# Combinations from kept scaled activations, a gate read by halves, adaLN in lots of eight and another order of the last down tiles in a two-layer trunk

## The chip, the core and the metric

The kernel runs on one core of one Trainium2 chip. The metric is the device time of one execution in microseconds; a profile of one execution stands beside it. The engines are TensorE (PE in the rows; PEld is its weight load), VectorE (DVE), ScalarE (ACT), GpSimd (POOL) and SyncE (SP), which issues all DMAs. On-chip buffers are SBUF tiles and, for TensorE's results, PSUM banks, here two accumulators of two banks each (`acc`) and four single banks (`aux`).

## The reference, cut to what matters

Two layers act on 512 prompt positions and 8 decode positions, 520 columns of width 1024, all in fp32. Each layer has an FFN at half weight, a mixing of a gated delta rule with windowed attention, and a second FFN. Each of the three begins with an RMS norm with shift and scale and ends with a gate; the nine vectors per layer come from a conditioning vector:

```python
m = jax.nn.silu(c) @ w_ada + b_ada                      # adaLN: 9 x 1024 per layer
h = rms_norm(x, g) * (1.0 + scale) + shift              # _modulate
x = x + 0.5 * gate * ((silu(h @ w_g) * (h @ w_u)) @ w_down)     # FFN, d_ff = 2816
h = modulate(x); x = x + gate * (mix(h @ w_in) @ w_out)         # mixing
```

The prompt has one set of the nine vectors for all its positions, the decode rows have one each.

## The kernel before

**Numbers and tiles.** x lies with its width on the partitions: 8 tiles k of 128 rows, each with 520 columns. The columns come in two halves (`HALF`): half 0 has 256 prompt columns, half 1 has 256 prompt and 8 decode columns, 264. Every fp32 matrix product is done as three matmuls on rounded parts: the high part of one factor by the high part of the other and the two mixed terms (`mmk`). So each activation h has a tile `hh` and a tile `hl` (high and low), one set for each half, and each 128x512 piece of a weight a `whi`, made by ScalarE, and a `wlo`, made by VectorE. Loads of 128x1024 (`raw`, a ring of four) and these pieces (a ring of eight) are run by `Stream`.

**Order.** There is no loop on the chip. The program is written out by one planner: `Clock` keeps an estimated time for each engine, and `Fill` holds side jobs written as generators (a norm, the combinations, adaLN lots), and starts a step of one of them between matmuls when the estimate says that its inputs are ready. The cost figures in `Ops` (lines 315 to 361) only decide this order. Every engine then executes its own row of instructions in that order, and waits where the first in the row waits.

**An FFN** (`ffn`, line 789). The norm of its input (`Norm`) makes `rs` from the sum of squares `ss`, one half at a time, and then for each of the 8 tiles k: VectorE forms t = x·g·rs, ScalarE rounds t + shift to `hh`, and VectorE forms `hl`. t alternates between two borrowed buffers, so the rows show them as `sq` and `ss`. For half 1 the 8 decode columns are done ahead of all this (`hs`). `head` (line 656) then makes the first two gate tiles and the first two up tiles in the plain way: 96 matmuls on half 0 into the accumulators, and 96 on half 1 into the four `aux` banks. The products of the other columns of d_ff, 128 gate columns and 128 up columns at a time, are made with a two by two scheme of seven products instead of eight (`seven`; 78 of them in the program). It needs sums of weights (GpSimd, `sum`, four per seven), and it needs combinations of h over the two halves and over tiles k and k + 4: for h1 = (tile k of half 0, of half 1) and h2 = (tile k + 4 of both),

```python
y0 = [h1[1] - h1[0],  h2[1] - y0[0]]
y1 = [h2[1] - h1[1],  h2[0] - y0[1]]
```

with k from 0 to 3. `combine` (line 762) makes them. GpSimd first adds `hh` and `hl` to a full h (`h32`; 4 operations of 128x264 per k), VectorE forms the four differences, ScalarE rounds y0 and y1 to `th` and VectorE forms their low parts `th`. `head` gives the job a turn after each of its 32 products. In `ffn` the results of `head` then go to `gate`, which reads an accumulator and an aux bank of each of its tiles; `seven` takes two aux banks and half of an accumulator.

The 22 tiles of d_ff are worked in two parts of 11 (`PARTS`), each with its sevens and then a down stage, in which the products with w_down are added to x. In the second part the last two tiles of x (y and z, numbers 6 and 7) are done by `tail` (line 722) with the halves apart, so that the norm of the next sub-layer can begin with half 0. It takes them as (0, y), (1, y), (0, z), (1, z), where the first number is the half. Its 11 tiles of d_ff make 33 matmuls per item.

**adaLN** (`ada_gen`, line 489) is a side job. One vector needs two lots of eight 256 KB loads, so four groups of four loads; the job keeps two groups in flight. The four products of a group show in the trace as one row of 8 records (`aux<-ada,sc`), and after the fourth group ScalarE copies the bank (`ada_sb`), TensorE transposes it and VectorE adds it up into `mt`. Outside the sevens it takes an aux bank; during them (`pairs`) it takes an accumulator for its whole vector.

## Time and profile before

| | us |
|---|---|
| median of three runs | 2313.55 |
| lowest and highest of them | 2308.82 and 2315.8 |
| the profiled execution's own time | 2309.65 |
| its span, from first to last instruction | 2307.9 |
| TensorE busy in it | 2158.9 (94%) |
| VectorE busy | 1657.3 (72%) |
| ScalarE busy | 1116.8 (48%) |
| GpSimd busy | 627.4 (27%) |

The mean granted clock of TensorE is 0.970 of full speed. A row of a timeline gives the start, the duration, the engine, the line and operation, the tile written and the tiles read, and the count of like instructions taken together; in brackets behind it stands the time that the engine was idle before it, and what ended that. Matmuls overlap, so their durations (0.28 us) are longer than the distance from one to the next.

### The profile page before, as it was taken

Reading aid. Unit: us, or ns where it says so; the run is one execution under the profiler, and the core shown is the slowest. Engines: PE = TensorE matmul, PEld = TensorE weight load, DVE = VectorE, ACT = ScalarE, POOL = GpSimd, SP = SyncE. Lnnn points to the kernel's source line nnn. Section 1 sums busy time; section 2 is a strip of 40 time slices with the busy share of each in tenths; the row PEclk is TensorE's granted clock in tenths of the full one; section 3 lists DMA queues with packets and bytes.
Section 4 is the critical chain, followed back from the end, with each engine's and each line's share of the span. In section 5 each row is a group of like instructions: output and inputs, shape, how many; then the busy total and the mean of one; then the engine's idle time right before and its main releaser. Section 6 shows DMA issues by size and latency. Waiting matters only on the chain.

```text
span 2307.9 us, 44270 instructions
## 1 busy us (share of the span) xinstructions
PE 2158.9 (94%) x17218; PEld 2018.2 (87%) x17218; DVE 1657.3 (72%) x3278; ACT 1116.8 (48%) x2438; POOL 627.4 (27%) x451
## 2 busy tenths in 40 slices
PE   7899999999988979999996999999999888899999
PEld 5789889989977868987996999999988777899999
DVE  5874687566877887567749956965677769974982
ACT  4453355356744445334534644643657444652651
POOL 0540452000111244044304614610001203532630
PEclk8999999999999989999997999999999998999999
DMA  8663454343223356358321333333432242233332
GB/s 277 231 223 105 175 182 140 110 78 104 85 74 118 124 177 216 110 205 303 105 93 46 97 105 95 98 107 98 87 108 67 79 131 74 84 107 94 93 109 75
DMA packets 177538, 287.79 MB, mean 125 GB/s; under 512 B 50448, under 2 KB 96176, under 8 KB 177328
## 3 DMA queue, kind: packets, MB, share of 16 engines
q1 hardware_dynamic: 177328, 284.96, 39.2%
q8 instruction: 135, 2.21, 0.4%
q14 instruction: 75, 0.61, 0.1%
HBM read 271.55 MB, written 14.41 MB: 124 GB/s over the span
## 4 chain that ended last, share of the span: by engine, by line
PE 79%; DVE 13%; ACT 4%; issue 2%; DMA 1%; SPq 0%; POOL 0%; DVEq 0%; ACTq 0%
PE aux L317 40%; PE acc L317 38%; DVE y L352 2%; DVE wlo L352 2%; DVE hl L352 1%; DVE sq L352 1%; ACT whi L344 1%; PE aux L327 1%; DVE th L352 1%; DVE ss L352 1%; ACT sq L344 1%; DVE g L352 1%; ACT s L344 1%; DVE s L352 1%; DVE x L352 1%
## 5 line engine op out<-in xcount | busy, mean ns | idle before, releaser
L344 ACT ACTIVATE whi<-raw 128x512 fp32r<-128x512 f32 (+1 forms) x594 | 360.1, 615 | 427.1 <-PE acc L317 303.2
L352 DVE TENSOR_TENSOR wlo<-raw,whi 128x512 fp32r<-128x512 f32 (+1 forms) x594 | 431.8, 744 | 71.8 <-ACT whi L344 71.2
L361 POOL TENSOR_TENSOR sum<-raw 128x512 f32<-128x512 f32 x156 | 247.2, 1585 | 848.3 <-DMA raw<-in_gu 664.1
L317 PE MATMUL aux<-th,whi 128*128 128x264 f32 (+1 forms) x2496 | 467.5, 286 | 3.7 <-ACT u L344 3.6
L317 PEld LDWEIGHTS aux<-th,whi 128*128 128x128 f32 x2496 | 384.8, 188 | 27.3 <-issue 13.4
L317 PE MATMUL aux<-th,wlo 128*128 128x264 f32 (+1 forms) x1248 | 353.3, 283 | 0.0
L352 DVE TENSOR_TENSOR wlo<-sum,whi 128x512 fp32r<-128x512 f32 x312 | 335.3, 1106 | 19.0 <-ACT whi L344 16.6
L317 PE MATMUL acc<-hh,whi 128*128 128x256 f32 x1256 | 326.0, 301 | 19.0 <-DVE x L352 14.7
L317 PE MATMUL acc<-hl,whi 128*128 128x256 f32 x1256 | 306.3, 285 | 6.7 <-DVE hl L352 6.3
L317 PE MATMUL acc<-hh,wlo 128*128 128x256 f32 x1256 | 305.9, 285 | 6.7 <-DVE wlo L352 6.7
L317 PE MATMUL aux<-hl,whi 128*128 128x264 f32 x928 | 269.2, 290 | 32.0 <-DVE hl L352 32.0
L317 PE MATMUL aux<-hh,whi 128*128 128x264 f32 x928 | 273.0, 294 | 11.8 <-ACT g L344 11.8
L317 PE MATMUL acc<-ghi,whi 128*128 128x256 f32 (+1 forms) x1320 | 272.4, 282 | 7.9 <-DVE t L352 7.9
L317 PE MATMUL acc<-glo,whi 128*128 128x256 f32 (+1 forms) x1320 | 272.0, 282 | 0.0
L317 PE MATMUL acc<-ghi,wlo 128*128 128x256 f32 (+1 forms) x1320 | 271.8, 282 | 0.0
L317 PE MATMUL aux<-hh,wlo 128*128 128x264 f32 x928 | 268.4, 289 | 0.0
L317 PEld LDWEIGHTS acc<-hh,whi 128*128 128x128 f32 x1256 | 220.3, 192 | 54.5 <-issue 37.0
L352 DVE SCALAR_TENSOR_TENSOR x<-acc,mt,x 128x256 f32<-128x256 f32 x136 | 61.6, 480 | 244.2 <-PE acc L317 244.2
L317 PEld LDWEIGHTS aux<-th,wlo 128*128 128x128 f32 x1248 | 234.8, 188 | 0.0
L317 PEld LDWEIGHTS acc<-hl,whi 128*128 128x128 f32 x1256 | 219.3, 192 | 8.3 <-DVE hl L352 7.9
L317 PEld LDWEIGHTS acc<-hh,wlo 128*128 128x128 f32 x1256 | 219.2, 191 | 8.1 <-DVE wlo L352 8.0
L344 ACT ACTIVATE whi<-sum 128x512 fp32r<-128x512 f32 x312 | 193.9, 623 | 46.6 <-PE acc L317 43.1
(318 smaller groups left out, 4014.4 us busy)
## 6 DMA issues: line engine op xcount, KB each, us to landing
raw<-in_gu SPq DMA_DIRECT2D x176, 512.0 KB, 3.6
...
```

Of the source, the lines that this page charges most:

```text
L317: self.nc.tensor.matmul(out, lhsT=lhsT, rhs=rhs, start=start, stop=stop, skip_group_check=join)
L327: self.nc.tensor.transpose(out, in_, ident)
L344: self.nc.scalar.activation(**k)
L352: getattr(self.nc.vector, f)(**k)
L361: getattr(self.nc.gpsimd, f)(**k)
```

## The change

1. **Combinations.** `Norm` of an FFN keeps t of all eight tiles and both halves (`ht`, 128x2x264), instead of overwriting it. Eight columns of half 0, which have no prompt position, are zero, and the eight decode columns of half 1 hold hs less the prompt's shift. `combine` forms differences of these t on GpSimd (three operations per k: y0[0], d, y1[1]) as soon as tile k + 4 of half 1 has its t (`norm.made`), and VectorE adds the shifts in two `stt` per k (y0[1], y1[0]) when the whole norm is done. The `h32` tiles are gone.
2. **The gate of the head.** `head` takes a generator `early`, which does the activation and the product of half 0 while half 1's matmuls run; half 1 follows in `gate_rest`, its splitting to high and low parts later. The first two sevens use the head's accumulators. A seven otherwise takes one aux bank and a whole accumulator. `head` offers `combine` a turn after every second product.
3. **adaLN.** Lots of eight loads instead of four, and always an aux bank. The side job may now go on in the down stage of the first part (`spares`).
4. **The last down tiles** come as (0, y), (0, z), (1, y), (1, z).
5. The planner's cost of GpSimd rises from 0.0019 to 0.003 us per column.

```diff
-        self.clk.run("pool", 0.1 + 0.0019 * self.cols(k["out"]), [k["out"]], self.aps(k, ("in_", "in0", "in1")))
+        self.clk.run("pool", 0.1 + 0.003 * self.cols(k["out"]), [k["out"]], self.aps(k, ("in_", "in0", "in1")))
...
-    def ada_load(l, g, h):
+    def ada_load(l, g):
         t = []
-        for k in range(4 * h, 4 * h + 4):
+        for k in range(KD):
             a = slot("ada", F32, (128, 512))
             dma(out=a, in_=ada[l, g, k])
...
+    def ada_mm(t, pa, u):
+        for k in range(KD):
+            r = 32 * (k % 4)
+            mm(pa[r:r + 32], lhsT=sc[:, u, k, :], rhs=t[k], start=u == 0 and k < 4, stop=u == 1 and k > 3, frac=0.27)
...
-            return len(used) + 4 <= SLOTS - 13
+            return len(used) + KD <= SLOTS - spares[0]
...
-            if not u and not h:
-                if pairs[0]:
-                    pa, pt = (acc()[:, i] for i in range(2))
-                else:
-                    pa, pt = aux(), None
-            ada_mm(t, pa, u, h)
-            if u and h:
+            if not u:
+                pa = aux()
+            ada_mm(t, pa, u)
+            if u:
                 m_sb = ada_out(pa)
                 yield m_sb,
...
             gg = mt[l][:, (3 * j + 1) * 8:(3 * j + 1) * 8 + 8, :]
-            t = [q[:, o:o + 256] for q in (self.sq, self.ss)]
+            keep = j != 1
+            if keep and a == 0:
+                self.ht = [slot("ht", F32, (128, 2, 264)) for _ in range(KD)]
+                for q in self.ht:
+                    pool("memset", out=q[:, 0, 256:264], value=0.0)
+            if keep:
+                t = [q[:, a, 0:256] for q in self.ht]
+            else:
+                t = [q[:, o:o + 256] for q in (self.sq, self.ss)] * 4
...
+                    if keep:
+                        for k in range(k0, k1):
+                            pool("tensor_tensor", out=self.ht[k][:, 1, 256:264], in0=hs[:, k - k0],
+                                 in1=sh[:, k, 0:1].to_broadcast([128, NS]), op=ALU.subtract)
+                elif keep:
+                    ops.copy(out=h8, in_=s0_)
+                    tt(out=l8, in0=s0_, in1=h8.bitcast(F32), op=ALU.subtract)
...
-    def head(norm, e=None):
+    def head(norm, e=None, early=None):
...
         norm.need(1, 0)
+        early = early(banks[0]) if early else None
         b1 = [aux() for _ in range(4)]
...
-                fill.try_(e)
+                if i % 2:
+                    fill.try_(e)
+            if early and k:
+                next(early, None)
...
     def combine(norm, th):
         for k in range(4):
-            yield lambda: norm.done[1] >= k + 5
-            h1, h2 = (slot("h32", F32, (128, 2, 264)) for _ in range(2))
-            for t, kk in ((h1, k), (h2, k + 4)):
-                for a in range(2):
-                    pool("tensor_tensor", out=t[:, a], in0=hh[a][0][:, kk, :].bitcast(F32),
-                         in1=hh[a][1][:, kk, :].bitcast(F32), op=ALU.add)
-            yield h1, h2
+            yield lambda: norm.made[1] >= k + 5
             y0, y1 = (slot("y", F32, (128, 2, 264)) for _ in range(2))
-            tt(out=y0[:, 0], in0=h1[:, 1], in1=h1[:, 0], op=ALU.subtract)
-            tt(out=y1[:, 0], in0=h2[:, 1], in1=h1[:, 1], op=ALU.subtract)
-            tt(out=y0[:, 1], in0=h2[:, 1], in1=y0[:, 0], op=ALU.subtract)
-            tt(out=y1[:, 1], in0=h2[:, 0], in1=y0[:, 1], op=ALU.subtract)
+            d = slot("d", F32, (128, 264))
+            h1, h2 = ht[k], ht[k + 4]
+            pool("tensor_tensor", out=y0[:, 0], in0=h1[:, 1], in1=h1[:, 0], op=ALU.subtract)
+            pool("tensor_tensor", out=d, in0=h2[:, 1], in1=h2[:, 0], op=ALU.subtract)
+            pool("tensor_tensor", out=y1[:, 1], in0=y0[:, 0], in1=d, op=ALU.subtract)
...
+        yield lambda: norm.done[1] >= KD
...
+            stt(out=y0[:, 1], in0=h2[:, 1], scalar=sh[:, k + 4:k + 5], in1=y0[:, 0], op0=ALU.add, op1=ALU.subtract)
+            stt(out=y1[:, 0], in0=h2[:, 1], scalar=ds[:, k:k + 1], in1=h1[:, 1], op0=ALU.add, op1=ALU.subtract)
...
+            pa, pb, pc = banks.pop(0) if banks else (None, aux(), None)
+            if pa is None:
                 u = acc()
-                unit.extend((u[:, 0], u[:, 1]))
-            pa = unit.pop(0)
+                pa, pc = u[:, 0], u[:, 1]
+            if pb is None:
+                pb, pc = aux(), aux()
...
+        def early(banks):
+            for i in range(0, 4, 2):
+                t = slot("g")
+                half.append(t)
+                act(out=t[:, 0:256], in_=banks[i], func=AF.Silu)
+                yield
+                tt(out=t[:, 0:256], in0=t[:, 0:256], in1=banks[i + 1], op=ALU.mult)
+                yield
+        def gate_rest(t, pg, pu):
+            act(out=t[:, 256:520], in_=pg, func=AF.Silu)
+            tt(out=t[:, 256:520], in0=t[:, 256:520], in1=pu, op=ALU.mult)
+            later(*split(t))
...
-                items = [(0, y, True, True, True), (1, y, False, False, True), (0, z, True, True, True), (1, z, False, False, True)]
+                items = [(0, y, True, True, True), (0, z, True, True, True), (1, y, False, False, True), (1, z, False, False, True)]
```

How the built kernels' rows differ is shown at three places. The first is VectorE in the head of the second FFN. Here `y` are the differences, `th` the low parts of the rounded ones, `wlo` low parts of weights, `hl` the low parts of h. Before, from the first combination's weights on:

```order
L352 TENSOR_TENSOR wlo_9578<-raw_9241,whi_9577 128x512
L352 TENSOR_TENSOR wlo_9581<-raw_9241,whi_9580 128x512
L352 TENSOR_TENSOR wlo_9587<-sum_9408,whi_9586 128x512
L352 TENSOR_TENSOR y_9620<-h32_9599 128x264
L352 TENSOR_TENSOR y_9621<-h32_9600,h32_9599 128x264
L352 TENSOR_TENSOR y_9620<-h32_9600,y_9620 128x264
L352 TENSOR_TENSOR y_9621<-h32_9600,y_9620 128x264
L352 SCALAR_TENSOR_TENSOR hl1_77<-sq_7639,mt0_80,hh1_76 128x256
L352 TENSOR_TENSOR th_9627<-y_9620,th_9626 128x528
L352 TENSOR_TENSOR th_9629<-y_9621,th_9628 128x528
L352 TENSOR_TENSOR y_9660<-h32_9651 128x264
```

After, from the last three `hl` on:

```order
L352 SCALAR_TENSOR_TENSOR hl1_77<-ht_9052,mt0_80,hh1_76 128x256
L352 SCALAR_TENSOR_TENSOR hl1_77<-ht_9053,mt0_80,hh1_76 128x256
L352 TENSOR_TENSOR dsh_9563<-mt0_80 128x4
L352 SCALAR_TENSOR_TENSOR y_9539<-ht_9050,mt0_80,y_9539 128x264
L352 SCALAR_TENSOR_TENSOR y_9540<-ht_9050,dsh_9563,ht_9046 128x264
L352 SCALAR_TENSOR_TENSOR y_9545<-ht_9051,mt0_80,y_9545 128x264
L352 SCALAR_TENSOR_TENSOR y_9546<-ht_9051,dsh_9563,ht_9047 128x264
L352 TENSOR_TENSOR th_9568<-y_9539,th_9567 128x528
L352 TENSOR_TENSOR th_9570<-y_9540,th_9569 128x528
L352 SCALAR_TENSOR_TENSOR y_9551<-ht_9052,mt0_80,y_9551 128x264
L352 SCALAR_TENSOR_TENSOR y_9552<-ht_9052,dsh_9563,ht_9048 128x264
L352 TENSOR_TENSOR th_9606<-y_9545,th_9605 128x528
```

The last two `hl` of half 1 stood between rows of the combinations (the second of them further on); now the first difference comes behind the last `hl`, and a `y` on VectorE reads `ht` instead of `h32`.

The second is GpSimd in the same head; before, `h32` is the sum of the two parts of h:

```order
L361 TENSOR_TENSOR h32_9512<-hh0_74,hl0_75 128x264
L361 TENSOR_TENSOR h32_9512<-hh1_76,hl1_77 128x264
L361 TENSOR_TENSOR h32_9513<-hh0_74,hl0_75 128x264
L361 TENSOR_TENSOR h32_9513<-hh1_76,hl1_77 128x264
L361 TENSOR_TENSOR sum_9584<-raw_9241,raw_9285 128x512
L361 TENSOR_TENSOR sum_9590<-raw_9241,sum_9408 128x512
L361 TENSOR_TENSOR h32_9599<-hh0_74,hl0_75 128x264
L361 TENSOR_TENSOR h32_9599<-hh1_76,hl1_77 128x264
L361 TENSOR_TENSOR h32_9600<-hh0_74,hl0_75 128x264
```

After, where `ht` are the kept scaled activations:

```order
L361 TENSOR_TENSOR ht_9053<-hs_9468,mt0_80 128x8
L361 TENSOR_TENSOR y_9539<-ht_9046 128x264
L361 TENSOR_TENSOR d_9541<-ht_9050 128x264
L361 TENSOR_TENSOR y_9540<-y_9539,d_9541 128x264
L361 TENSOR_TENSOR y_9545<-ht_9047 128x264
L361 TENSOR_TENSOR d_9547<-ht_9051 128x264
L361 TENSOR_TENSOR y_9546<-y_9545,d_9547 128x264
L361 TENSOR_TENSOR y_9551<-ht_9048 128x264
L361 TENSOR_TENSOR d_9553<-ht_9052 128x264
L361 TENSOR_TENSOR y_9552<-y_9551,d_9553 128x264
L361 TENSOR_TENSOR y_9557<-ht_9049 128x264
```

The four additions per k have become three subtractions, which stand in one row, ahead of the weight sums of the next seven.

The third is VectorE at the entry of the first mixing, behind the first FFN's last down tiles (`x` written from `acc` is half 0, from `aux` half 1). Before:

```order
L352 SCALAR_TENSOR_TENSOR x_73<-aux_5364,mt0_80,x_73 128x256
L352 TENSOR_TENSOR t8_5415<-aux_5364,mt0_80 128x8
L352 TENSOR_TENSOR x_73<-x_73,t8_5415 128x8
L352 TENSOR_TENSOR ss_4765<-ss_4765,sq_4766 128x264
L352 SCALAR_TENSOR_TENSOR x_73<-acc_5420,mt0_80,x_73 128x256
L352 TENSOR_TENSOR ss_4765<-ss_4765,sq_4766 128x256 x2
L352 TENSOR_TENSOR wlo_5409<-raw_5264,whi_5408 128x512
L352 SCALAR_TENSOR_TENSOR sq_4766<-x_73,mt0_80,rs_5484 128x256
L352 SCALAR_TENSOR_TENSOR ss_4765<-x_73,mt0_80,rs_5484 128x256
L352 SCALAR_TENSOR_TENSOR hl0_75<-sq_4766,mt0_80,hh0_74 128x256
```

After:

```order
L352 SCALAR_TENSOR_TENSOR x_73<-acc_5331,mt0_80,x_73 128x256
L352 TENSOR_TENSOR ss_4773<-ss_4773,sq_4774 128x256
L352 SCALAR_TENSOR_TENSOR x_73<-acc_5331,mt0_80,x_73 128x256
L352 TENSOR_TENSOR ss_4773<-ss_4773,sq_4774 128x256 x2
L352 TENSOR_TENSOR wlo_5333<-raw_5180,whi_5332 128x512
L352 SCALAR_TENSOR_TENSOR sq_4774<-x_73,mt0_80,rs_5437 128x256
L352 SCALAR_TENSOR_TENSOR ss_4773<-x_73,mt0_80,rs_5437 128x256
L352 SCALAR_TENSOR_TENSOR hl0_75<-sq_4774,mt0_80,hh0_74 128x256
L352 SCALAR_TENSOR_TENSOR sq_4774<-x_73,mt0_80,rs_5437 128x256
```

The second half-0 tile (`acc_5331`) now comes ahead of the first half-1 tile, and with it the first rows of half 0's norm (`sq` from `x` and `rs`).

## Rows read from the trace of the kernel before

**Rows 1.** The page's chain that ended last, shares of the span by engine.
```profile
PE 79%; DVE 13%; ACT 4%; issue 2%; DMA 1%; SPq 0%; POOL 0%; DVEq 0%; ACTq 0%
```

**Rows 2.** TensorE's waits: line, waited for: us in total, times, longest us.
```profile
PE aux L317 <- DVE hl L352: 32.0, 6, 8.5
...
PE aux L317 <- ACT g L344: 17.7, 3, 5.9
...
PE aux L327 <- ACT ada_sb L344: 8.0, 2, 7.3
...
PE acc L317 <- DVE t L352: 7.9, 7, 1.1
...
PE acc L317 <- DVE wlo L352: 6.7, 5, 3.8
...
PE acc L317 <- DVE hl L352: 6.3, 3, 2.4
```

**Rows 3.** Timeline of PE, head 2: start, us, operation, [idle before <-releaser].
```profile
812.31 0.59 PE L317 MATMUL aux<-hl,whi 128*128 128x264 f32 x1 [8.46 <-DVE hl L352]
...
817.65 0.59 PE L317 MATMUL aux<-hl,whi 128*128 128x264 f32 x1 [2.33 <-DVE hl L352]
...
826.33 1.94 PE L317 MATMUL aux<-ada,sc 128*32 128x512 f32 x8 [5.89 <-ACT g L344]
```

**Rows 4.** Windows of head 2: us, busy (records) by engine, PEclk, DMA share, GB/s.
```profile
794.80:804.00 9.20, 9.05 (x75) 8.84 (x73) 9.02 (x13) 2.26 (x5) 6.09 (x7) 1.00 0.03 10
812.30:820.50 8.20, 5.80 (x23) 5.18 (x23) 8.17 (x10) 1.88 (x4) 6.86 (x6) 0.50 0.04 14
835.00:845.00 10.00, 10.00 (x86) 8.88 (x88) 9.00 (x11) 5.55 (x12) 6.05 (x4) 1.00 0.87 315
```

**Rows 5.** Timeline of DVE, head 2.
```profile
790.67 0.23 DVE L352 TENSOR_TENSOR hs<-x,rs 128x64 f32<-128x64 f32 x1 [1.55 <-ACT rs L344]
...
810.29 0.42 DVE L352 TENSOR_TENSOR y<-h 128x264 f32<-128x264 f32 x1
...
820.73 1.49 DVE L352 TENSOR_TENSOR y<-h,h 128x264 f32<-128x264 f32 x1
...
826.03 0.42 DVE L352 TENSOR_TENSOR g<-g,acc 128x256 f32<-128x256 f32 x1 [0.98 <-ACT g L344]
...
830.19 1.32 DVE L352 TENSOR_TENSOR th<-y,th 128x528 fp32r<-128x528 f32 x2
```

**Rows 6.** Timeline of POOL, head 2, and its 128x8 memsets (line, busy, mean ns).
```profile
798.20 0.75 POOL L361 TENSOR_TENSOR h<-hh,hl 128x264 f32<-128x264 f32 x1 [3.11 <-DVE hl L352]
...
820.59 1.33 POOL L361 TENSOR_TENSOR sum<-sum,raw 128x512 f32<-128x512 f32 x1
...
L967 POOL MEMSET bt<- 128x8 f32 x2 | 0.2, 104 | 0.0
```

**Rows 7.** Timeline of PE, the last product on th of head 2's first seven.
```profile
837.76 0.28 PE L317 MATMUL aux<-th,wlo 128*128 128x264 f32 x1
```

**Rows 8.** Windows of the three entries behind an FFN, columns as in rows 4.
```profile
450.00:470.00 20.00, 14.13 (x98) 13.46 (x99) 17.67 (x44) 9.88 (x21) 0.00 (x0) 0.91 0.36 112
1204.90:1224.10 19.20, 15.33 (x116) 14.36 (x116) 16.60 (x36) 10.42 (x21) 2.97 (x4) 1.00 0.17 55
1591.70:1610.70 19.00, 14.44 (x101) 13.61 (x101) 17.03 (x44) 9.73 (x22) 0.00 (x0) 0.91 0.37 118
```

**Rows 9.** Timeline of PE, entry of the first mixing.
```profile
464.07 0.39 PE L317 MATMUL acc<-hh,wlo 128*128 128x256 f32 x1 [3.76 <-DVE wlo L352]
```

**Rows 10.** Timeline of DVE there, half 0's last hi/lo half.
```profile
459.38 0.48 DVE L352 SCALAR_TENSOR_TENSOR hl<-ss,mt,hh 128x256 fp32r<-128x256 f32 x1 [0.18 <-ACT hh L344]
```

**Rows 11.** Timelines of PE and ACT, adaLN's transposes in the first FFN.
```profile
94.85 1.11 PE L327 MATMUL aux<-cs,ada_sb 128*128 128x128 f32 x4 [7.31 <-ACT ada_sb L344]
...
94.22 0.58 ACT L344 ACTIVATE ada_sb<-aux 128x512 f32<-128x512 f32 x1
```

**Rows 12.** Timeline of SP, adaLN loads in the first FFN.
```profile
71.53 13.43 SPq L311 DMA_DIRECT2D ada<-in_ada  x16
```

100 lines of the change are left out of this document (63 added, 37 removed).

## The prediction

> **What bounds the kernel now.** I read the chain of waits first: it runs through TensorE for 79% of the span and through VectorE for 13% [rows 1]. So TensorE sets the time, and what can be won is its idle time and the stretches in which it runs slowly. The list of TensorE's waits comes next [rows 2]. The matrix products themselves are not changed in number, so only waits can go. Six lines of that list belong to places that the diff touches: hi/lo halves of h that VectorE hands over late (32.0 us in 6 waits), the gate's activation (17.7 us in 3), an adaLN copy (8.0 us), accumulators in the down stage (7.9 us in 7), a late weight half (6.7 us) and hi/lo halves at the entry of the mixing (6.3 us). Of these 78.6 us nearly all is within the edit's reach; the few small waits in the groups I leave.
>
> The three heads with a full queue (the second to fourth FFN) all look the same, which the counts 6 and 3 show. I take head 2. TensorE stands still for 8.46, 2.33 and 5.89 us [rows 3], and between and behind these waits it crawls: 12 matmuls lie between the starts at 812.31 and 817.65, so without the 2.33 us of waiting they take 3.01 us, 0.25 us each. In the stretch before the first wait 75 matmuls take 9.05 us, 0.121 each, at a granted clock of 1.00; in the stretch behind it the clock is 0.50, the lower of the two levels (1.2 GHz) [rows 4]. So after each idle time there is a further loss of some microseconds.
>
> Why TensorE waits: VectorE is the queue in front of it. From 790.67 (the first row of the second half's norm) to 826.03 (the gate's product) it is busy nearly without a break, 9.02 of 9.20 us and 8.17 of 8.20 us in two stretches [rows 4, 5], and the hi/lo half that TensorE waits for until 812.31 stands behind eight differences y, two halves th and three weight halves, as the order of the kernel before shows. Those rows are also slow: a y of 128x264 took 0.42 us at 810.29, while GpSimd had nothing to do, and 1.49 us at 820.73, while a sum of 1.33 us ran on GpSimd [rows 5, 6]. VectorE and GpSimd hinder each other there.
>
> **The heads.** The change takes 4 of 16 additions per head from GpSimd and 8 of 16 differences from VectorE, lets GpSimd begin when the scaled activations exist (not when both halves of h are split), and puts all 16 norm instructions ahead of the combinations. Now count VectorE's instructions. Before, 46 stand from the norm's first row to the gate's product, and they take 826.03 - 790.67 = 35.4 us, 0.77 each [rows 5]. After, the hi/lo halves of h are within the first 22, so the 96 matmuls of the second half, which need 96 x 0.121 = 11.6 us from 794.8, run through to about 806.4, without waiting for the aux buffers of the gate. The first thing that TensorE then needs from VectorE is the 35th instruction, a weight half (at 0.77 each: 817.6), and the last combination is the 44th: 790.7 + 44 x 0.77 = 824.5. The last 9 of the 36 products on it need 1.1 us; since TensorE will have idled from some 809 to 817 it restarts at the lower clock, and I allow 1 to 2 us more: 827. Before, these 36 products ended at 838.0 [rows 7]. That gives 11 us per head, 33 for three. This is the largest and the least certain term. The lower end: if GpSimd's twelve operations in a row hold VectorE back as at 820.73 most of the time, the mean rises to 1.0 us per instruction, the 44th ends at 834.7 and the head gains 1 to 2 us, 4 in all. The upper end: the rows are undisturbed, 0.55 us each, the 44th ends at 815, and TensorE (806.4 plus 12 + 12 + 36 matmuls at 0.121 and some 3 us for 16 adaLN records and the transposes, 10 us and a little) sets the end near 818: 20 per head, 60 in all. I choose the middle because the work per instruction stays mixed in the same way, and the measured mean contains the contention.
>
> The Trainium skill, page "SBUF — State Buffer", section "SBUF: two separate sides", says that the port pair shared by VectorE and GpSimd is an exclusive lock, so that a VectorE operation with two SBUF inputs and a GpSimd operation exclude each other for whole instructions. The 1.49 us beside 0.42 us agrees with that. The rule speaks against this change, since the new `stt` still read two SBUF operands and GpSimd's twelve operations now start amid the norm's sixteen. With full exclusion the undisturbed rows add up: 8 th at 0.66 and 36 others at 0.42 us on VectorE, 12 operations at 0.75 and six sums at 1.33 us on GpSimd [rows 5, 6], together 37.4 us; the last combination would stand at 828.1 instead of 824.5, and the time would be 11 us longer over three heads, 2261.
>
> The early gate of half 0 costs nothing on ScalarE, which is free for most of the head; it takes the 5.89 us wait apart, which is inside the count above. The extra 8 memsets and 8 tiny differences of 128x8 on GpSimd per norm stand ahead of the big ones; a memset of 128x8 takes 0.104 us [rows 6], so together under 2 us of a queue that has nothing else to do then. At the opening two more small VectorE operations per group: under 1 us.
>
> **The entries behind the FFNs.** Moving half 0's last tile ahead of half 1's lets half 0's norm start 33 matmuls earlier, 33 x 0.121 = 4.0 us. Before, in the three stretches between the end of the last down tile and the second half's first matmul, TensorE works 98, 116 and 101 records, at 0.121 us 11.9, 14.0 and 12.2 us, in 20.0, 19.2 and 19.0 us [rows 8]: losses of 8.1, 5.2 and 6.8, together 20.1. The largest single wait of the first is 3.76 us for a weight half that stood on VectorE behind half 1's first norm rows [rows 9]; the lower clock adds to it (0.91 in the mean). The last hi/lo half of half 0 ends at 459.86 [rows 10]; 4 us earlier it ends near 456, and the first half, which wants it at 450.0 + 7 x 1.43 = 460.0, does not wait. The weight half now stands ahead of half 0's last rows. In its place the last two hi/lo halves of half 1 stand behind three weight halves that wait for buffers which half 1's fourth step frees; each row of that kind takes 0.48 us [rows 10], so I count 0 to 1 us an entry. I count 20.1 - 3 = 17. Lower end 6, if VectorE, 17.67 of 20.00 us busy there [rows 8], only changes which half is late; upper end 20.
>
> **The first FFN.** TensorE's transposes wait 7.31 us for an adaLN copy on ScalarE that stands at 94.22 behind four copies y to th, which wait for VectorE [rows 11]. After, no such copy stands between others that wait, and the products come later than the copies. The wait goes, with some of the lower clock behind it. Against that, the loads come in one row of 24 at about 0.84 us each (16 took 13.43 us [rows 12]), and the first lot of eight may land 2 us after TensorE wants it. I count 6.5; ends 0 and 9.
>
> **The down stage of the first FFN.** Seven waits of 1.13 us, 7.9 in all [rows 2], are for one accumulator less: the adaLN lot in flight held one of the two, and now it takes an aux buffer. I count 7; the ends are 4 (two lots that now run in this stage keep TensorE waiting 2 us each, about two of these waits) and 7.9.
>
> **Sum.** 33 + 17 + 6.5 + 7 = 63.5 us. The profiled execution took 2309.65 us, the median of the runs is 2313.55. From the profiled one this gives 2246, from the median 2250. I forecast 2250. The lower ends add to 14, the upper to 97; they will not fall together.
>
> **Rivals.**
> (1) The wait at the heads only moves: TensorE stops waiting for h and waits as long for a combination or a weight half. For it: VectorE was full, and only 2 of 46 instructions leave the row before the last combination. Against: eight differences and four additions are gone. It gives 4 for 33: 2279. Chance 0.13.
> (2) The heads run undisturbed, 60 for 33: 2223. Chance 0.10; the contention in [rows 5] speaks against it.
> (3) Slower: weights late behind lots of eight. SP issues all loads in one order, and a lot is now 8 x 256 KB, 2.1 MB, which at the 315 GB/s of a busy stretch [rows 4] takes 6.7 us, 3.3 longer than half a lot. If each of the 32 lots keeps TensorE 3.3 us longer from a weight, that is 106 us, and the time is 2250 + 106 = 2356; from 20 lots on (63.5 / 3.3 = 19.2) the change is slower than before. For it: the DMA engines are 0.87 busy in that stretch. Against: 16 loads in a row are issued now too [rows 12], the list of TensorE's waits has no wait for a raw weight, and the total of bytes is the same. Chance 0.05.
> (4) The entries gain nothing but the order: 6 for 17, and the opening 0 for 6.5: 2267. Chance 0.12.
> That the new order does not come about is no rival: the order of the built kernel shows it.
>
> **How the numbers follow.** The forecast's own case, 2238 to 2264, has 0.60, the rivals 0.40. The range 2226 to 2282 leaves out the slow rival, half of rival 2 and a little beyond rival 1, some 0.15 to 0.2. What a measurement of this kernel can tell from no change is 0.3%, 7 us. Every case but the third is faster by more than that, and a mix of the lower ends (14) with a mild form of rival 3 would lie within it: faster 0.91, same 0.04, slower 0.05.
>
> **What would show it.** Right: in head 2 no wait for `hl` among the 96 matmuls of the second half, one wait of 5 to 10 us before the products on th, and these ending 9 to 13 us sooner relative to the second half's start; no seven waits on `t`; no 7.31 us for `ada_sb`; entries of 12 to 14 us. Wrong: new waits for `ada` or raw loads by DMA among TensorE's waits (rival 3), a wait for `th` as long as the three of before (rival 1), or y rows on VectorE well over 1 us. What I don't see from here is what the changed planner cost does to later stages of the mixing; I take that as nothing.

## The result and the profile after

The changed kernel took 2285.43 us (median of four runs, 2283.64 to 2285.63), the kernel before 2311.95 on the same occasions: a ratio of 0.9883, with an interval of 0.9866 to 0.9900. The change gains 27 us, less than half of the 63.5 that were forecast, and the time lies 3.4 us above the upper end of the range. The profiled execution took 2285.49 us, at a mean granted clock of 0.979; against the profiled one of before it is 24.2 us shorter (23.8 between the marks used below).

From the page of the changed kernel, the busy time of each engine and the chain that ended last:

```profile
PE 2155.7 (94%) x17218; PEld 2022.2 (89%) x17218; DVE 1602.5 (70%) x3264; ACT 1119.0 (49%) x2438; POOL 603.5 (26%) x499
...
PE 76%; DVE 16%; issue 3%; ACT 3%; DMA 1%; SPq 0%; POOL 0%; DVEq 0%; ACTq 0%
```

VectorE has 55 us less work than before (1657.3), GpSimd 24 less. Yet VectorE's share of the chain rose from 13% [rows 1] to 16%: where TensorE waits, it still waits for VectorE's row. TensorE's waits in the changed kernel (waited for: us in total, times, longest us), to be read beside [rows 2]:

```profile
PE acc L317 <- DVE x L352: 17.6, 12, 3.5
PE acc L317 <- ACT u L344: 15.9, 10, 11.6
...
PE acc L317 <- DVE g L352: 12.8, 15, 3.1
PE acc L317 <- ACT g L344: 9.2, 1, 9.2
PE acc L317 <- DVE hl L352: 8.1, 5, 3.7
PE acc L317 <- DVE wlo L352: 7.9, 4, 3.7
PE aux L317 <- DMA ada<-in_ada: 6.4, 1, 6.4
...
PE aux L317 <- DVE hl L352: 2.7, 4, 1.4
...
PE aux L327 <- ACT ada_sb L344: 0.7, 1, 0.7
```

The old names are nearly gone: `aux <- hl` fell from 32.0 to 2.7 us, `ada_sb` from 8.0 to 0.7, and the seven waits on `t` do not appear. New names have come: ScalarE's copies `u` and `g`, and VectorE's product `g` 15 times. The largest entry, for `x`, stood in the list of before with 14.7 us in 8; four waits of 0.7 us have been added, one in each tail. (The 6.4 us for `ada` is the opening's, which before had one of its own of 6.3.)

To see where the time went I cut both traces at marks that exist in both and compared the distances, in us:

| part | forecast | before to after |
|---|---|---|
| heads of the second, third, fourth FFN | -33 | -6.4, -5.1, -6.2: -17.7 |
| three entries behind an FFN | -17 with the next | -7.3, -2.2, -5.9: -15.3 |
| four tails | | +1.4, -0.3, +0.9, +1.2: +3.2 |
| head of the first FFN, from its start to the last product on th | -6.5 | +0.2 |
| sevens and first down stage of the first FFN | -7 | -9.2 |
| late part of the two mixings, up to the next norm | 0 | +8.7, +4.9: +13.5 |
| sevens and first down stage, second FFN | 0 | -3.8 |
| the same, third and fourth FFN | 0 | +3.6, +1.8: +5.3 |
| all else | 0 | -0.1 |
| sum | -63.5 | -23.8 |

Each distance is from one execution of each kernel; some vary by 2 to 4 us, as the experiments show. Of the 39.7 us that are missing, the heads account for 15.3, the late mixings for 13.5, the first FFN's head for 6.7, entries and tails for 4.9, and the sevens nearly cancel (-0.7).

**Heads.** VectorE did what was forecast and a little more. In head 2 the row from `hs` (784.50) to the last `th` (end 815.22) takes 30.7 us; 33.8 were forecast up to the last combination. In heads 3 and 4 it takes 30.9 and 31.8. The ends of that row in head 2, on VectorE:

```profile
784.50 0.23 DVE L352 TENSOR_TENSOR hs<-x,rs 128x64 f32<-128x64 f32 x1 [2.91 <-ACT rs L344]
...
813.90 1.32 DVE L352 TENSOR_TENSOR th<-y,th 128x528 fp32r<-128x528 f32 x2
```

But the end of the products on th came not 2.5 us after it, as allowed, but 10.3, 9.5 and 8.1 us. None of the 36 products started before the last combination was made, and in head 3 TensorE stood idle until then. Timelines of the changed kernel, first PE and then ACT and DVE, around that wait:

```profile
1221.40 0.27 PE L317 MATMUL acc<-hh,wlo 128*128 128x256 f32 x1
1233.29 0.81 PE L317 MATMUL acc<-th,whi 128*128 128x264 f32 x2 [11.61 <-ACT u L344]
...
1236.77 0.81 PE L317 MATMUL acc<-th,whi 128*128 128x264 f32 x2 [0.48 <-ACT u L344]
```

```profile
1227.13 1.18 ACT L344 ACTIVATE th<-y 128x528 fp32r<-128x528 f32 x2 [2.01 <-DVE y L352]
1229.18 1.18 ACT L344 ACTIVATE th<-y 128x528 fp32r<-128x528 f32 x2 [0.87 <-DVE y L352]
...
1232.34 0.62 ACT L344 ACTIVATE ghi<-g 128x520 fp32r<-128x520 f32 x1
1232.86 0.37 ACT L344 ACTIVATE u<-acc 128x264 f32<-128x264 f32 x1
```

TensorE's next product writes an accumulator that ScalarE must empty first (`u`). That copy needs nothing from VectorE: its product was done at 1221.7. But it stands in ScalarE's row behind copies `th<-y`, and each row of those waits for VectorE's `y`. So the row that was to be hidden is waited for in full here. The forecast counted VectorE's row and TensorE's work, and ScalarE as "free for most of the head"; free it is, but not free to go on. In heads 2 and 4 the longest waits are 2.09 and 3.13 us for the gate's `g`, which VectorE and ScalarE make behind rows of the combinations. The 24 plain products of the first seven follow these waits (in head 2 with adaLN products between them, in head 4 mostly at the lower clock), and the products on th come last.

ScalarE is not the only reason. In `seven` the 36 products stand on TensorE as three runs of 12, and each run goes through all four combinations. So 26 of the 36 stand behind the last combination's low part, not 9. The kernel before shows the same: its last `th` of head 2 ends at 831.51 [rows 5], and the first product on th (PE, before) starts behind that. They end 6.5 us after the last `th` in head 2 and 5.1 in heads 3 and 4, so 2.5 us was too little by the trace of before already.

```profile
832.31 0.41 PE L317 MATMUL aux<-th,whi 128*128 128x264 f32 x2
```

Two smaller things in the same places. A weight half now waits behind norm rows of half 1 at the start of heads 2 and 4; and after each such wait TensorE runs at the lower clock. PE and DVE of the changed kernel, start of head 2, and two windows (us, busy (records) by engine, PEclk, DMA share, GB/s): the 6 us behind this wait, and the 5 us behind the wait of 11.61:

```profile
788.83 0.58 PE L317 MATMUL acc<-hh,wlo 128*128 128x256 f32 x1 [3.68 <-DVE wlo L352]
```

```profile
787.54 1.23 DVE L352 TENSOR_TENSOR wlo<-raw,whi 128x512 fp32r<-128x512 f32 x1
```

```profile
788.80:794.80 6.00, 5.97 (x28) 5.98 (x29) 6.00 (x10) 2.03 (x4) 4.16 (x5) 0.50 0.92 344
1233.30:1238.30 5.00, 4.52 (x19) 4.21 (x20) 5.00 (x9) 2.71 (x6) 0.16 (x1) 0.50 0.40 119
```

28 matmuls in 6.0 us are 0.21 each, against the 0.121 at full clock.

**First FFN.** The wait for `ada_sb` [rows 11] is gone, and one of 9.24 us for the gate's `g` ends 13 us earlier. Timelines of PE, ACT, DVE and POOL of the changed kernel:

```profile
81.48 0.80 PE L317 MATMUL acc<-hh,whi 128*128 128x256 f32 x2 [9.24 <-ACT g L344]
```

```profile
72.48 0.64 ACT L344 ACTIVATE th<-y 128x528 fp32r<-128x528 f32 x1 [1.80 <-DVE y L352]
73.97 0.64 ACT L344 ACTIVATE th<-y 128x528 fp32r<-128x528 f32 x1 [0.85 <-DVE y L352]
78.73 0.64 ACT L344 ACTIVATE th<-y 128x528 fp32r<-128x528 f32 x1 [4.11 <-DVE y L352]
80.23 0.64 ACT L344 ACTIVATE th<-y 128x528 fp32r<-128x528 f32 x1 [0.85 <-DVE y L352]
80.78 0.65 ACT L344 ACTIVATE g<-acc 128x256 f32<-128x256 f32 x2
```

```profile
68.08 0.48 DVE L352 SCALAR_TENSOR_TENSOR y<-ht,dsh 128x264 f32<-128x264 f32 x1
...
77.21 1.49 DVE L352 SCALAR_TENSOR_TENSOR y<-ht,mt,y 128x264 f32<-128x264 f32 x1
78.62 1.51 DVE L352 SCALAR_TENSOR_TENSOR y<-ht,dsh 128x264 f32<-128x264 f32 x1
```

```profile
78.48 1.36 POOL L361 TENSOR_TENSOR sum<-sum,raw 128x512 f32<-128x512 f32 x1
```

It is the same pattern as in head 3: an activation whose input is ready stands behind copies that wait for VectorE, and VectorE's rows take three times their undisturbed 0.48 us, as long as the sums on GpSimd beside them.

**Late mixing.** Behind the first mixing's middle a wait of 3.68 us for `hl` is new. PE and DVE of the changed kernel:

```profile
701.79 0.39 PE L317 MATMUL acc<-hl,khi 128*128 128x256 f32 x1 [3.68 <-DVE hl L352]
```

```profile
697.72 1.14 DVE L352 SCALAR_TENSOR_TENSOR s<-bv,misc,s 128x128 f32<-128x128 f32 x4 [2.12 <-DMA bv<-vnd]
...
699.21 2.19 DVE L352 TENSOR_SCALAR s<-s,sm 128x256 f32<-128x256 f32 x8
701.32 0.42 DVE L352 TENSOR_TENSOR hl<-o,hh 128x256 fp32r<-128x256 f32 x1
```

The low half stands behind rows of a decode-attention job (`s`) that wait for a load. In the kernel before this job came later, and the wait does not exist. None of the five points of the change speaks of the mixing. One line of `Norm` that the diff above leaves out does bear on it: `drop(hs)`, which gives the buffer of the decode columns back to the pool, in the mixing's norm as well. e1 and e11 test it.

**Entries.** Windows of the three entries in the changed kernel, columns as above, beside [rows 8]:

```profile
442.30:455.30 13.00, 12.19 (x100) 11.71 (x99) 11.93 (x33) 5.98 (x14) 0.00 (x0) 1.00 0.67 210
1191.80:1205.30 13.50, 12.11 (x99) 11.64 (x98) 12.65 (x31) 7.20 (x14) 6.24 (x11) 1.00 0.39 118
1572.30:1585.20 12.90, 12.03 (x98) 11.56 (x98) 11.84 (x33) 5.87 (x14) 0.00 (x0) 1.00 0.66 210
```

Counted as in the prediction, by records at 0.121 us, TensorE loses 0.9, 1.5 and 1.0 us there instead of 8.1, 5.2 and 6.8 [rows 8], at full clock.

**Tails.** The new order puts the half-0 products of y and z next to each other, and `tail` makes them in the two halves of one accumulator. In each tail TensorE now waits once for VectorE's `x` of y, for 0.7 us, which makes 2.8 of the 3.2 us. In the first (PE of the changed kernel):

```profile
429.74 0.36 PE L317 MATMUL acc<-ghi,whi 128*128 128x256 f32 x1 [0.67 <-DVE x L352]
```

### The profile page after: what moved, and what is told of

It reads as the page before. It is cut to its first block, busy times and chain, and to the rows that moved or that the text cites. A ratio compares the mean times of both kernels' runs of the same rounds, so it can differ in the third digit from the quotient of the medians.

```text
span 2283.7 us, 44328 instructions
## 1 busy us (share of the span) xinstructions
PE 2155.7 (94%) x17218; PEld 2022.2 (89%) x17218; DVE 1602.5 (70%) x3264; ACT 1119.0 (49%) x2438; POOL 603.5 (26%) x499
## 4 chain that ended last, share of the span: by engine, by line
PE 76%; DVE 16%; issue 3%; ACT 3%; DMA 1%; SPq 0%; POOL 0%; DVEq 0%; ACTq 0%
PE acc L317 46%; PE aux L317 29%; DVE wlo L352 4%; DVE g L352 2%; DVE s L352 2%; DVE hl L352 1%; DVE y L352 1%; PE aux L327 1%; DVE th L352 1%; DVE u L352 1%; ACT sq L344 1%; DMA bv<-vnd 1%; DVE ht L352 1%; DVE cy L352 1%; DVE t L352 1%
## 5 line engine op out<-in xcount | busy, mean ns | idle before, releaser
L317 PE MATMUL acc<-hh,whi 128*128 128x256 f32 (+1 forms) x1568 | 417.6, 299 | 36.1 <-DVE x L352 14.9
L317 PE MATMUL acc<-hh,wlo 128*128 128x256 f32 (+1 forms) x1568 | 397.2, 287 | 8.2 <-DVE wlo L352 7.9
L317 PE MATMUL acc<-hl,whi 128*128 128x256 f32 (+1 forms) x1568 | 397.1, 286 | 2.6 <-DVE hl L352 2.5
L317 PE MATMUL aux<-th,whi 128*128 128x264 f32 (+1 forms) x1824 | 340.7, 284 | 0.0
L317 PEld LDWEIGHTS aux<-th,whi 128*128 128x128 f32 x1824 | 281.3, 188 | 4.2 <-issue 4.2
L317 PE MATMUL aux<-th,wlo 128*128 128x264 f32 (+1 forms) x912 | 258.1, 283 | 0.0
L317 PEld LDWEIGHTS acc<-ghi,whi 128*128 128x128 f32 x1320 | 206.9, 188 | 16.8 <-issue 15.9
L317 PEld LDWEIGHTS acc<-glo,whi 128*128 128x128 f32 x1320 | 207.4, 188 | 0.0
L317 PEld LDWEIGHTS acc<-ghi,wlo 128*128 128x128 f32 x1320 | 207.1, 188 | 0.0
L317 PE MATMUL aux<-hl,whi 128*128 128x264 f32 x616 | 175.6, 285 | 2.8 <-DVE hl L352 2.7
```

The costliest lines, as they stand in the source:

```text
L317: self.nc.tensor.matmul(out, lhsT=lhsT, rhs=rhs, start=start, stop=stop, skip_group_check=join)
```

## Experiments

My theory after the two traces: (a) the mixing's loss comes from a buffer that is given back earlier, not from the planner's cost of GpSimd; (b) in the first FFN and in the heads TensorE waits for ScalarE copies that stand behind `th<-y`, and VectorE's row decides when they get through; (c) in the sevens of the second layer two results share one accumulator. The rival for (b) is that the end of a head is set by TensorE itself, by late weight halves and the lower clock; for the heads also that the lots of eight or the order of the tail are to blame. All times are medians of four runs, all ratios are to the kernel before. Distances between marks are from one profiled execution each, and the late part of the first mixing varied from 143.5 to 147.9 us among the profiles of kernels that have the same order there; 147.9 is the changed kernel's own. Head 2 varies too: e4 leaves the first layer's order as it is, and has 44.8 us there against 42.6. A difference of some 2 us in head 2, or 4 us in the first late mixing, says nothing by itself.

### e1 and e11: the buffer of hs

```diff
-                    drop(hs)
+                    if keep:
+                        drop(hs)
```

> The changed kernel, except that the mixing's norm no longer gives its small tile hs back to the pool (one line; before, hs was never given back). Theory: the late mixing (from the first XT product to the norm of the second FFN) is 8.7 and 4.9 us longer than before because one free tile more lets the planner admit a decode job of the window attention earlier, so other steps of the delta rule and its output wait behind it on VectorE. Then this run restores the old order there and gains about 13 us: 2272 us, with the stretch from XT to the norm's sum back at 139 us in each layer (after: 147.9 and 144.4). Rival: those steps are late because VectorE or GpSimd get there later for another reason (the planner's cost of GpSimd, the earlier entry); then the time stays at 2285 us within 2 us.

e1 keeps the buffer in the mixing's norm, as before. It took 2272.11 us (0.9825, 0.9810 to 0.9841). The late parts take 138.5 and 141.7 us, against 147.9 and 144.4 in the changed kernel and 139.2 and 139.6 before, and the planner's new cost of GpSimd is in it. e11 is the converse, on the kernel before:

```diff
                     tt(out=lo[:, k0:k1, 256:264], in0=hs, in1=hi[:, k0:k1, 256:264].bitcast(F32), op=ALU.subtract)
+                    drop(hs)
```

> The kernel before with one line added: the norm gives its small tile hs back to the pool. Theory: this alone brings the changed kernel's order of the late mixing, and the stretch from the first XT product to the norm's sum grows from 139.2 and 139.6 us by 4 to 9 and 3 to 5 us: 2319 to 2326 us. Rival: the longer late mixing of the changed kernel needs its other edits too; then this is 2312 us within 2 us.

It took 2329.12 us (1.0071, 1.0053 to 1.0089): this line alone makes the kernel before 16 us slower. The late parts take 145.2 and 144.6 us. Beyond that the second FFN's sevens became 8 us longer, where waits of 1.13 us on `t`, like those of the first FFN [rows 2], now stand too. So (a) holds from both sides: one free buffer more lets the planner start a decode-attention job earlier, and its rows stand ahead of what TensorE waits for. On VectorE e1 has the order of before again there, and e11 that of the changed kernel. The cost figure is not the cause.

### e2: the gate ahead of the combinations in the first FFN

```diff
-            e = fill.add(combine(norm, th), 0.5)
+            e = fill.add(combine(norm, th, lambda k: k < 2 or len(ghi) > k), 0.5)
```

Inside `combine`, the new condition is waited for ahead of each k; it is passed in the first FFN only.

> The changed kernel, except that in the first FFN the third and fourth combination are held back until the gates of the third and fourth tile are written out, so that these activations stand ahead of the copies y to th on ScalarE. Theory: the wait of 9.24 us at 72.2 (accumulator held by a gate whose activation stands on ScalarE behind four copies that wait for VectorE) goes, the next wait is for th before the first seven, and the first FFN up to its first product on th is 5 to 9 us shorter: 2277 to 2281 us. Rival: VectorE's 1.5 to 1.7 us rows beside GpSimd's sums are the limit wherever the gate stands; then the wait moves to the first product on th and the time stays at 2285 us within 2 us.

2273.58 us (0.9831, 0.9812 to 0.9850). The first products on th come 9.0 us earlier, and 3.3 are given back in the first down stage. On ScalarE the gate now stands at 70.50 and nothing waits ahead of it (timeline of ACT, e2):

```profile
69.46 1.14 ACT L344 ACTIVATE whi<-raw 128x512 fp32r<-128x512 f32 x2
70.50 0.64 ACT L344 ACTIVATE g<-acc 128x256 f32<-128x256 f32 x2
```

The work is the same and only its order on ScalarE and VectorE differs, so the order is the cause in the first FFN. The profile has about 4 us less in the late mixings (145.2 and 142.9 us), which this edit doesn't touch; that is within their spread.

### e3, e5, e6, e7: four edits to the heads

e3 makes the early gate of half 0 in one go, e5 lets the weight halves go ahead of half 1's norm rows, e6 puts the two results of the first seven into different accumulators, and e7 places the wait for all combinations after the first seven's plain products.

```diff
-        early = early(banks[0]) if early else None
+        if early:
+            for _ in early(banks[0]):
+                pass
+            early = None
```

> The changed kernel, except that the half-0 activation and product of the head's two gates are written out before half 1's matmuls instead of between them, so that on VectorE the two products stand 6 and 15 places further ahead. Theory: in the second and fourth head TensorE's 2.1 and 3.1 us waits for the gate's product, and the 1.5 us one behind it, are waits for the accumulators of the first seven; they go, with 1 to 2 us of lower clock behind them, and each of these heads ends 3 to 4 us earlier: 2278 to 2280 us. Rival: the last combination (th at 815 in the second head) sets the end of these heads whatever stands ahead; then TensorE only waits later and the time stays at 2285 us within 2 us, or rises by 1 to 2 us because the differences y come later.

```diff
                 mmk(banks[0][i], ws[(k // 4) * 4 + i], k % 4, h_src, k, 0, k == 0, k == KD - 1)
+                if not k:
+                    W.rest()
```

> The changed kernel, except that in the head the eighth weight half is written out right after the first step of half 0, so that it stands on VectorE ahead of half 1's norm. In the second and fourth head the changed kernel has a new wait of 3.68 us for it, and with the lower clock behind it half 1 starts 7.3 us later after the norm's sum than before (13.1 against 5.8 us). Theory: VectorE's row from the norm to the last combination sets the end of these heads, so the time won at half 0 is waited for again in front of the first seven: half 1 starts 5 to 7 us earlier, the products on th end 0 to 2 us earlier, the time is 2281 to 2285 us. Rival: the late start is what cost the heads their gain; then each of the two ends 6 to 7 us earlier, 2272 us.

```diff
-            banks.extend(((v[:, 0], u[:, 0], u[:, 1]), (v[:, 1], None, None)))
+            banks.extend(((v[:, 0], u[:, 0], v[:, 1]), (u[:, 1], None, None)))
```

> The changed kernel, except that the first seven behind a head keeps its two alternating results in two different accumulators (its third shares the tile with the second's half that is read earliest). Theory: the four waits of 0.48 us for ScalarE's copy u and 0.60 us for the gate between this seven's products come from the two results lying in one accumulator tile; they go in the second to fourth head, 2.0 us each: 2279 us, and the 36 products on th take 4.7 to 5.2 us in a row where the clock is high instead of 6.1 to 8.2. Rival: the waits are real dependences of the alternation; then nothing changes: 2285 us.

```diff
             tt(out=t0, in0=pa[:, 0:256], in1=u1[:, 0, 0:256], op=ALU.add)
+            fill.until(lambda: len(th) == 4)
             prod(pb, 264, of_t(0, 1), False)
...
-                fill.until(lambda: len(th) == 4)
```

> The changed kernel, except that the first seven behind a head is written out up to its second product before the planner waits for the combinations, so that in the third head ScalarE's copy of the first product, u, stands ahead of the last copies y to th (in the other heads the order hardly changes). Theory: in the third head all 36 products on th come after the last combination, because the first of them needs that copy, and the copy stood on ScalarE behind all eight copies to th and four weights; with the copy ahead the products on the first three combinations run while the fourth is made, and the 11.6 us wait shrinks to 6 to 9 us, the head ends 2 to 5 us earlier: 2280 to 2283 us. Rival: the first combination itself is that late; then the time stays at 2285 us within 1 us.

| kernel | us | ratio | heads 2, 3, 4 (us; after: 42.6, 36.2, 41.5) |
|---|---|---|---|
| e3 | 2281.01 | 0.9866 (0.9851 to 0.9880) | 44.4, 35.8, 42.3 |
| e5 | 2278.92 | 0.9861 (0.9846 to 0.9876) | 42.7, 35.0, 41.5 |
| e6 | 2277.01 | 0.9852 (0.9836 to 0.9869) | 44.6, 34.5, 41.3 |
| e7 | 2281.15 | 0.9872 (0.9852 to 0.9891) | 44.7, 35.4, 41.1 |

A head is counted here up to the last product on th: heads 2 and 4 from the last sum of squares, head 3 from half 1's first matmul. All four intervals overlap that of the changed kernel (0.9866 to 0.9900), and in all four most of the difference lies in the late mixings and in the second FFN's sevens; so the parts must decide.

In e3 the waits of 2.1 and 3.1 us for VectorE's `g` are 0.6, but waits for ScalarE of 3.8 and 2.8 us came in heads 2 and 4; no head ended sooner beyond the spread, so its theory fails. e5 decides on late weight halves and the lower clock behind them: with the weight half ahead, half 1 starts 6.6 us earlier in heads 2 and 4 (6.49 instead of 13.13 us behind the mark), TensorE has no wait of 3.68 us there and a granted clock of 1.00, and the heads end where they ended (in head 4 to 0.1 us; in head 2 within the spread of 2). So the late weight half and the lower clock behind it were not on the path. The wait only moved: the list of e5 has

```profile
PE acc L317 <- ACT u L344: 23.1, 11, 12.1
```

e7 tells how much of head 3 is ScalarE's. There `u` stands ahead of the last copies to th, and the products on th begin 3.6 us earlier in the head; the head ends only 0.8 earlier. PE of e7:

```profile
1229.17 0.81 PE L317 MATMUL acc<-th,whi 128*128 128x264 f32 x2 [8.01 <-ACT u L344]
...
1232.63 0.59 PE L317 MATMUL acc<-th,whi 128*128 128x264 f32 x1 [0.21 <-DVE th L352]
...
1234.98 0.81 PE L317 MATMUL acc<-th,whi 128*128 128x264 f32 x2 [1.54 <-ACT u L344]
```

The first run of 12 waits for the last combination, and the two other runs come behind it, largely at the lower clock. VectorE's row itself took 32.5 us instead of 30.9. e6 removes the pauses of 0.48 us between the products on th: 8.23 us for the 36 became 6.58 in head 3, with some 1 us more behind it; in heads 2 and 4 that figure hardly changed (6.1 and 6.3), as one wait for `g` (1.2 and 0.9 us) takes their place.

### e9: VectorE's row without GpSimd's reads

```diff
-            pool("tensor_tensor", out=y0[:, 0], in0=h1[:, 1], in1=h1[:, 0], op=ALU.subtract)
-            pool("tensor_tensor", out=d, in0=h2[:, 1], in1=h2[:, 0], op=ALU.subtract)
-            pool("tensor_tensor", out=y1[:, 1], in0=y0[:, 0], in1=d, op=ALU.subtract)
+            pool("memset", out=y0[:, 0], value=0.0)
+            pool("memset", out=d, value=0.0)
+            pool("memset", out=y1[:, 1], value=0.0)
```

> The changed kernel, except that GpSimd's three differences per combination are memsets of the same tiles, which read nothing; so the combinations are left out of the computation in part (y0 and y1 hold only what VectorE adds). Theory: VectorE's rows in the heads are slow (0.97 us for a 128x256 row that takes 0.48 us alone) while GpSimd reads and writes SBUF beside them; with memsets the row from the half-1 norm to the last combination, 30.7 to 31.8 us in the second to fourth head, falls by 4 to 6 us, and the heads end 3 to 6 us earlier each: 2269 to 2276 us. Rival: the weight sums, which stay, do the same; then the row falls by under 2 us and the time is 2281 to 2285 us.

2262.67 us (0.9785, 0.9771 to 0.9800). VectorE has the same instructions, and its row takes 24.7 us instead of 30.7 in head 2 and 25.7 instead of 31.8 in head 4. In head 2 of the changed kernel, DVE and then POOL:

```profile
790.67 0.97 DVE L352 SCALAR_TENSOR_TENSOR ht<-x,mt,rs 128x256 f32<-128x256 f32 x1
791.56 0.97 DVE L352 SCALAR_TENSOR_TENSOR hl<-ht,mt,hh 128x256 fp32r<-128x256 f32 x1
```

```profile
790.48 0.87 POOL L361 TENSOR_TENSOR d<-ht 128x264 f32<-128x264 f32 x1 [2.26 <-DMA ada<-in_ada]
```

The same place in e9:

```profile
781.28 0.48 DVE L352 SCALAR_TENSOR_TENSOR ht<-x,mt,rs 128x256 f32<-128x256 f32 x1
781.68 0.48 DVE L352 SCALAR_TENSOR_TENSOR hl<-ht,mt,hh 128x256 fp32r<-128x256 f32 x1
```

```profile
781.27 0.57 POOL L359 MEMSET y<- 128x264 f32 x2
```

The twelve differences cost VectorE 6 us in heads 2 and 4, and 2 in head 3 (30.9 to 28.7). The heads end 3.3, 2.5 and 6.5 us sooner (42.63 to 39.30, head 3 with its entry 49.77 to 47.25, 41.46 to 34.99), together 12.3; the rest of the 22.8 us by which e9 is faster than the changed kernel lies in the first late mixing (4.3, within its spread), the first FFN and the sevens. Shortening VectorE's row shortens the heads, which e5 could not. So VectorE's row decides, as (b) says; ScalarE's part in (b) is shown by e2 in the first FFN, and is small in head 3 by e7. The Trainium skill, page "SBUF — State Buffer", section "SBUF: two separate sides", says that a VectorE operation with two SBUF inputs is locked out only by a GpSimd operation that reads SBUF. Both halves of that agree here: 0.97 us beside differences, 0.48 us beside memsets.

### e4: accumulators in the sevens of the second layer

```diff
+            if l and not banks:
+                u = acc()
+                banks.extend(((u[:, 0], None, None), (u[:, 1], None, None)))
             pa, pb, pc = banks.pop(0) if banks else (None, aux(), None)
...
             spares[0] = 4
+            banks.clear()
```

> The changed kernel, except that the sevens of the second layer (in which no adaLN lots run) take two aux banks and half of an accumulator again, as before, apart from the first two behind a head. Theory: the sevens of the third and fourth FFN are 3.6 and 2.9 us longer than before because two results of a seven now lie in one accumulator tile, and the second of them waits for VectorE's read of the first (rows of 0.6 us, wait for DVE g); then this gives back 5 to 6 us: 2279 to 2280 us, and the waits acc<-th for DVE g fall from 15 to 6 or fewer. Rival: these sevens are slower for what they inherit from the head (weights and gates late); then the time stays at 2285 us within 2 us.

In the second layer this restores the half accumulator per seven of before; the first layer keeps the changed banks. 2280.61 us (0.9864, 0.9849 to 0.9879; the interval overlaps the changed kernel's), and the parts in question fall by 3.0 us in the third FFN and 1.8 in the fourth. The waits for `g`, of some 0.6 us each, are fewer (list of e4; 15 in the changed kernel):

```profile
PE acc L317 <- DVE g L352: 10.9, 10, 3.6
```

So giving a seven a whole accumulator, which leaves an aux bank for the adaLN lots of the first layer, has a price where no such lots run.

### e8: the old order of the last down tiles

```diff
-                items = [(0, y, True, True, True), (0, z, True, True, True), (1, y, False, False, True), (1, z, False, False, True)]
+                items = [(0, y, True, True, True), (1, y, False, False, True), (0, z, True, True, True), (1, z, False, False, True)]
```

> The changed kernel with the old order of the last down tiles, (0, y), (1, y), (0, z), (1, z). Theory: the entries behind the first three FFNs (from the start of the second down stage to half 1's first matmul) lose again what they won, 5.9, 2.5 and 4.9 us by the two traces, and the rest stays: 2297 to 2300 us. Rival: with the norms kept apart otherwise (half 0's shift columns, kept activations), the entries depend on VectorE's load more than on the order; then 2285 to 2290 us.

2294.16 us (0.9923, 0.9908 to 0.9937). The entries take 21.0, 21.1 and 18.8 us instead of 13.0, 13.5 and 12.9: 21.5 us in all. The total moves by only 9 us. In the third FFN the 7.6 us at the entry come back within the head (28.0 + 8.2 us become 21.9 + 6.5), since VectorE's row sets its end whenever half 1 starts: the row begins 9.6 us behind the tail and takes 31.8 (9.4 and 30.9 in the changed kernel). In the tails 2.5 us come back, as the waits for `x` go; 4 us less in the late mixings are within their spread. Heads 2 and 4 take 45.0 and 41.0 us, so the order of the tail is not what holds them up. The order is worth about what was forecast for the two mixings, and nothing in the third FFN.

### e12: lots of four

e12 has the groups of four loads of before, on an aux bank as in the changed kernel:

```diff
-        for k in range(KD):
+        for k in range(4 * h, 4 * h + 4):
             a = slot("ada", F32, (128, 512))
...
-            return len(used) + KD <= SLOTS - spares[0]
+            return len(used) + 4 <= SLOTS - spares[0]
```

> The changed kernel with adaLN's loads and products in lots of four again, still in an aux bank and still admitted in the first part's down stage. Theory: the size of the lots is nearly neutral; the seven waits of 1.13 us in the first FFN's down stage went because the lots left the accumulators, so none of them comes back, and the weights were not late behind lots of eight: 2283 to 2288 us, and the sevens and down stages of the first two FFNs together within 3 us of the changed kernel's. Rival: lots of eight keep weights waiting somewhere (the third rival of the prediction in a mild form); then lots of four give 5 us or more, 2280 us or less.

2291.09 us (0.9913, 0.9896 to 0.9929). The sevens and the first down stage of the first FFN take 269.1 us in e12 and 268.6 in the changed kernel, so the seven waits went by the aux bank, not by the size of the lots. The second FFN's take 308.0 against 301.4. Lots of eight hold nothing up; if anything they gain a few us. The heads take 43.3, 36.0 and 42.0 us with lots of four, so the lots do not hold them up either. Rival 3 falls: the changed kernel's list has no wait of TensorE for a weight load.

### e10: four mends together

e10 is the changed kernel with the edits of e1, e2, e4 and e6.

> The changed kernel with four mends together: hs kept in the mixing's norm (e1), the first FFN's gates ahead of the later combinations (e2), the two banks of the first seven apart (e6), the old banks of the sevens in the second layer (e4). Theory: the four losses lie in different stretches and add: 11 + 9 + 6 + 5 = 31 us below the changed kernel, 2254 us; with what the second and sixth share with neighbours 2254 to 2260. Rival: stretches behind give back what is won ahead (the adaLN lots of the first FFN, the third and fourth head behind VectorE's row); then 2265 us or more.

2260.85 us (2254.39 to 2262.71), a ratio of 0.9772 (0.9752 to 0.9793): faster than both kernels, 24.6 us below the changed one and just above the range expected. Singly the four gave 13.3 + 11.9 + 4.8 + 8.4 = 38.4. Much of the difference is probably counted more than once: in their profiles e2, e4 and e6 had shorter late mixings, by 4.3, 2.7 and 4.7 us, without touching them. No run separates this. What is left in its list at the heads is what these mends do not reach:

```profile
PE acc L317 <- ACT u L344: 11.6, 1, 11.6
PE acc L317 <- DVE g L352: 9.1, 9, 2.3
```

## Why the prediction was wrong

**Heads, 33 forecast, 17.7 measured.** The count of VectorE's row was right and rather too long (33.8 us forecast, 30.7 to 31.8 measured), 0.70 us per instruction instead of 0.77; the 37.4 us added up for full exclusion did not come. The step that failed is "the last 9 of the 36 products on it need 1.1 us … I allow 1 to 2 us more". It assumed that 27 products would have been made by then. None had. The end came 8 to 10 us after the row, not 2.5: 6 to 8 us more per head, less the 2 to 3 by which the row was shorter, which makes 12 of the missing 15.3. The runs show three parts of it. First, only ten of the 36 can stand ahead of the last combination's low part, by their order on TensorE; in the kernel before, too, they all came behind and ended 5.1 to 6.5 us after it. Second, the 36 took 6.1 to 8.2 us instead of 36 x 0.121 = 4.4, with pauses of 0.48 us for `u` (gone in e6) and in part at the lower clock. Third, they began 1.3 to 4.2 us after the row, behind ScalarE's copy `u` in head 3 and behind plain products in heads 2 and 4 that had waited for `g`. How the 12 us divide among the three is not shown; putting `u` ahead gave 0.8 us in head 3 (e7). Rival 1 named this direction (a wait of the same length at another name) with a gain of 4; what happened lies between it and the forecast. The path stated for it, a full VectorE, was right (e9). Of the marks given for "right" in head 2, there is no `hl` wait in the 96 matmuls; the one wait of 5 to 10 us before the products on th is two of 2.1 and 1.7 us (11.6 in head 3); and these products end 13.7 us sooner after half 1's start, more than the 9 to 13 named, but half 1 itself starts 7.4 us later after the sum of squares. That mark could not show the loss.

**The wait that the change adds at a weight half** (3.68 us in heads 2 and 4, and the slow 6 us behind it) was not in the forecast at all. Taking it away gave the heads nothing, by e5.

**Entries, 17 forecast with what follows, 12.1 measured.** The three entries lost 15.3 us and stand at 12.9 to 13.5 us, as forecast (12 to 14). Two steps were off: the third FFN's share (2.2 instead of 5.2) was not to be had by this edit, as e8 shows, and the tails became 3.2 us longer, mostly by the waits for `x`, which I had left out. The loss of one engine at an entry counts only if the next stage does not wait for another.

**First FFN.** For its head 6.5 were forecast and 0 came. The statement "no such copy stands between others that wait" held for the adaLN copy and failed for the gate's activation, some 13 us earlier in the same row: the planner placed four copies ahead of it (by which of its changes is not shown). e2 gives the size of that, 9 us. The down stage's 7 was right (9.2 measured), and its reason too: the seven waits are gone, and e12 shows that the size of the lots did not do it.

**Late mixing, 0 forecast, +13.5 measured.** This was the sentence "what the changed planner cost does to later stages of the mixing; I take that as nothing". The place was right, the cause was not: it is the buffer of `hs` that goes back to the pool. The diff ahead of the prediction leaves that line out. It gave a job an earlier start in a stage that the change does not speak of. The built order differs there, and the prediction reads only the rows of the heads and entries.

**Sevens of the second layer, 0 forecast, +5.3 measured** (4.7 of them by e4): I counted the accumulator that a seven gets in full as a gain where it was scarce, and gave it no price elsewhere.

**Range.** Its lower ends added up to a gain of 14, and the measured 24 to 27 lies between that and the sum; the range left this out because the lower ends were held to be independent. That they have a cause in common, rows that free accumulators behind VectorE's, is likely in part. But the mixing's 13.5 us lay outside every end: with that one line put back (e1) the time is 2272 us, inside the range. So two things failed together, the term put at nothing for the mixing and the heads' 2.5 us.
